# Small reciprocal-root chains on the Vector engine in other forms, and five instead of three output tiles multiplied in halves of the tokens at a change of stage

## The chip, the cores and the metric

The kernel runs on one core of a Trainium2 chip. The metric is the device time of one execution in microseconds (us). Five engines with a program each share the core's SBUF: TensorE (PE, with PEld for its weight loads), VectorE (DVE), ScalarE (ACT), GpSimd (POOL) and SyncE (SP, which issues transfers). PE writes its results to PSUM.

## The reference

512 tokens of width 1024 pass through two layers (mixer, then a feed-forward network) and a second block (attention, then a feed-forward network). All in fp32:

```python
def rms_norm(x, g):
    y = xf * lax.rsqrt(jnp.mean(xf * xf, axis=-1, keepdims=True) + EPS)
    return y * g
for l in range(2):
    h = rms_norm(x, g_pre_mix[l]) * (1 + sc_mix) + sh_mix
    x = x + gt_mix * rms_norm(mixer(h, ...), g_post_mix[l])
    h = rms_norm(x, g_pre_mlp[l]) * (1 + sc_mlp) + sh_mlp
    f = square(relu(h @ w_ff1[l])) @ w_ff2[l]          # 1024 -> 4096 -> 1024
    x = x + gt_mlp * rms_norm(f, g_post_mlp[l])
# second block
h = rmsnorm(x, attn_norm_w);  x = x + attention(h)
h2 = rmsnorm(x, mlp_norm_w);  x = x + square(relu(h2 @ w_up)) @ w_down
return rmsnorm(x, final_norm_w)
```

## The kernel before

**Products.** A product of fp32 matrices is made from three matmuls of rounded parts (`mm3`, L202 to L204): high by high, high weight by low activation, low weight by high activation. Weights come in chunks of 128x1024: a transfer into a raw buffer (`wr`, two of them), a rounded high part by ACT (L178), and the low part as the difference, by DVE in one piece or by POOL in four (L182). The pair goes to one of four `w` buffers. `W()` hands out the next chunk and prepares chunks up to four ahead; a fifth has to wait until the first of the four is used up.

**Change of stage.** A mixer or a feed-forward network ends in `tok_group`: four accumulators (tiles `p`), one for each group of 128 tokens, added to `E` by DVE as each gets its last product. Then `post_norm` takes the groups in pairs (or singly, where `pt=1`: the end of the first feed-forward network). For each pair: squares summed (ACT L580), multiplied by a gate row (POOL L582), a first chain of small DVE operations (`rsqrt`, all of it at L69 with tiles named `c`), the update `E += E*c` (DVE), squares again (ACT L593), a second chain, the scaling (ACT L460, DVE), 16 transposes on PE (L475) two blocks to a PSUM bank, eviction (DVE and ACT L485), and the split into high (ACT L214) and low parts (DVE) `hT`. The next stage multiplies weights by `hT`.

`rsqrt` is a bit-trick guess and two correction steps, in 128x`w` operations: `w` is 2 for a pair, 1 for a single group. A chain of `w=2` has 9 operations, one of `w=1` has 7.

**Halves.** At the head of a stage `feat` takes several output tiles of 128 columns at once:

```python
for _ in evacs: ws.append(self.W()...)
for i, _ in enumerate(evacs):
    bs.append(self.bank(tag="py" if halves and i >= 3 else tag))
for a, b in ([(0, 256), (256, 512)] if halves else [(0, 512)]):
    if a:
        self.work_off()                 # transposes of the second pair
    for w, p, ev in zip(ws, bs, evacs):
        for k in range(8):
            self.mm3(p[:, a:b], ...)    # 24 matmuls of 256 columns
```

so the first 256 tokens of all these tiles are multiplied before the second pair of groups is there. The number of tiles is `HALVES` in the three feed-forward networks (`self.feat([ev] * HALVES, halves)`) and in the second mixer; the first mixer and the second block begin otherwise. The remaining tiles are multiplied 512 tokens wide. A scheduler sorts the instructions of each engine from priorities and its own clock of the work issued, so that an edit also moves neighbours.

The five changes of stage are at 431 us (first mixer to first network), 807 (network to second mixer), 1197 (mixer to network), 1575 (network to second block) and 1977 (second block to last network).

Of the kernel before, what the change touches and what calls it, by code (L numbers as in the profile page):

```python
# [10 lines left out]
I32 = mybir.dt.int32  # L11
AFTER = mybir.DependencyInfo(mybir.DependencyClass.NoSync, mybir.DependencyReason.DATA)
AF = mybir.ActivationFunctionType
OP = mybir.AluOpType

T, D, DFF = 512, 1024, 4096
NL, NH, DH = 2, 4, 256
KC, KM = 31, 4
EPS = 1e-6
AHEAD = 4  # L20
HALVES = 3
MID = 3
PIECE = 256
CALM = True
# [22 lines left out]
RSQRT_C, RSQRT_GUESS = 1.5 ** 0.2, 0x5f05a21f  # L47
# [25 lines left out]
class Kern:  # L73
# [148 lines left out]
            nc.scalar.activation(hi, src, AF.Copy if isinstance(scale, float) else AF.Identity, scale=scale)  # L222
            self.V.scalar_tensor_tensor(lo, src, scale, f32(hi), op0=OP.mult, op1=OP.subtract)

    def rsqrt(self, src, w, mul, add, tag=None):

        V = self.V
        vh, z, q, y1, y = (self.c(w, tag) for _ in range(5))

        def half_square(z):  # L230
            a = self.c(w, tag)
            if w == 1:
                V.scalar_tensor_tensor(a, z, vh, z, op0=OP.mult, op1=OP.mult)
            else:
                V.tensor_tensor(a, z, z, op=OP.mult)
                V.tensor_tensor(a, a, vh, op=OP.mult)
            return a
        V.tensor_scalar(vh, src, 0.5 * mul, 0.5 * add, op0=OP.mult, op1=OP.add)
        V.tensor_scalar(z.bitcast(I32), vh.bitcast(I32), -0.5, RSQRT_GUESS, op0=OP.mult, op1=OP.add)
        h = half_square(z)  # L240
        V.scalar_tensor_tensor(q, h, -RSQRT_C ** 2 * 5 / 3, h, op0=OP.add, op1=OP.mult)
        V.scalar_tensor_tensor(y1, q, RSQRT_C ** 4 * 5 / 4, z, op0=OP.add, op1=OP.mult)
        a = half_square(y1)
        V.scalar_tensor_tensor(y, a, 1.5, y1, op0=OP.subtract, op1=OP.mult, reverse0=True)
        return y
# [199 lines left out]
        for ev, b in zip(evacs, bs):  # L445
            ev(b)

    def norm_T(self, ii, xs, ss, G, sh, to):

        V, w = self.V, len(xs)  # L450
        if ii == 0:
            self.new_hT()
        r = self.rsqrt(ss, w, 1.0 / D, EPS)
        for b in range(2):
            h = slice(512 * b, 512 * b + 512)
            for t in range(w):
                if (t if w > 1 else b):
                    V.tensor_scalar(to[t][:, h], xs[t][:, h], r[:, t:t + 1], None, op0=OP.mult)
                else:
                    self.nc.scalar.activation(to[t][:, h], xs[t][:, h], AF.Copy, scale=r[:, t:t + 1])  # L460
        self.xn += to
        if len(self.xn) == 2:
            i, x, self.xn = ii + w - 2, self.xn, []
            for q in range(4):
                self.pend.append((i, lambda q=q: self.norm_T2(i, q, x, G, sh)))
# [92 lines left out]
    def post_norm(self, l, which, nxt):  # L558

        nc, V = self.nc, self.V  # L560
        self.ada_wait(l, range(16 + 24 * which, 24 + 24 * which))
        row = self.gate_row(l, which)
        GS = nxt()
        self.n += 1
        dst = self.dram.tile([T, D], F32, name=f"xd{self.n}")
        src = self.xsrc
        self.xsrc = [dst[i * 128:(i + 1) * 128, :] for i in range(4)]
        xs, ss, w = [None] * 4, {}, 1 if self.tune["pt"] else 2

        def ready(i, nh):  # L570
            y, t = self.y[i], i % w
            self.calm = nh == 1 and CALM
            h = slice(nh * 512, (nh + 1) * 512)
            if nh == 0:
                xs[i] = self.tile("E", (128, D))
                nc.sync.dma_start(xs[i], src[i])
                if t == 0:
                    ss[i // w] = self.c(2 * w)
            with self.soon():
                nc.scalar.activation(self.tile("j", (128, 512), BF16), y[:, h], AF.Square,  # L580
                                     accum_out=ss[i // w][:, w * nh + t:w * nh + t + 1])
                nc.gpsimd.tensor_tensor(y[:, h], y[:, h], row[:, h], op=OP.mult)  # L582
            return (lambda: update(i - t)) if nh and t == w - 1 else None

        def update(i):
            with self.soon():
                s, s1, s2 = ss[i // w], self.c(w), self.c(w)
                V.tensor_tensor(s1, s[:, 0:w], s[:, w:2 * w], op=OP.add)
                r = self.rsqrt(s1, w, 1.0 / D, EPS)
                for t in range(w):  # L590
                    n, x = i + t, xs[i + t]
                    V.scalar_tensor_tensor(x, self.y[n], r[:, t:t + 1], x, op0=OP.mult, op1=OP.add)
                    nc.scalar.activation(self.y[n].bitcast(BF16)[:, 0:D], x, AF.Square, accum_out=s2[:, t:t + 1])  # L593
                    nc.sync.dma_start(self.xsrc[n], x)
                    self.dbg(f"x{l}{which}_{n}", x)
                self.norm_T(i, xs[i:i + w], s2, *GS, self.y[i:i + w])
        return ready


# [280 lines left out]
    def mixer(self, l, nxt, halves=True):  # L880
        nc, V = self.nc, self.V
        o, _ = COLS["w_conv_m"]
# [7 lines left out]
        def ev_xm(j):  # L890
            def ev(p):
                if j % 2 == 0:
                    xmt[j // 2], xct[j // 2] = (self.tile("E", (128, 2, T)) for _ in range(2))
                xm, xc = xmt[j // 2][:, j % 2], xct[j // 2][:, j % 2]
                nc.scalar.activation(xm, p, AF.Copy)
                y, th = p, self.t2()
                w = lambda d: self.cols[l][:, o + j * KM + KM - 1 - d:o + j * KM + KM - d]
                nc.scalar.activation(y, p, AF.Identity, scale=w(0), bias=self.col(l, "b_conv_m", j))
                for d in range(1, KM):
                    V.scalar_tensor_tensor(y[:, d:], xm[:, :T - d], w(d), y[:, d:], op0=OP.mult, op1=OP.add)  # L900
                nc.scalar.activation(th, y, AF.Tanh)
                V.scalar_tensor_tensor(xc, th, 1.0, y, op0=OP.add, op1=OP.mult)
            return ev
# [4 lines left out]
        def ev_gb(c):  # L908
            def ev(p):
                th = self.t2()  # L910
                nc.scalar.activation(th, p, AF.Tanh, scale=0.5)
                self.drain(lambda: c - self.taps_done < self.bufs["ga"])
                a = self.tile("ga", (128, T))
                V.scalar_tensor_tensor(a, th, 1.0, ga["a"], op0=OP.add, op1=OP.mult)
                inp[c] = a
            return ev
# [11 lines left out]
        glu = lambda c: self.feat([ev_ga]) or self.feat([ev_gb(c)])  # L928
        z = lambda j: self.feat([ev_z(j)])
        nh = HALVES  # L930
        gw = self.gate_weights(l)
        rest = lambda: [0 for _ in gw]
        if halves:
            next(gw), next(gw)
            self.feat([ev_xm(j) for j in range(nh)], halves, rest)
            glu(0)
        else:
            nh = 2
            self.start([ev_xm(0), ev_xm(1), ev_ga, ev_gb(0)])
            self.load_cols(1)  # L940
# [21 lines left out]
        hms, ss = [], {}  # L962
# [696 lines left out]
```

## Time and the profile before

| | |
|---|---|
| median of 3 runs | 2338.77 us (2337.93 to 2339.65) |
| profiled execution | 2338.5 us, of it the span 2336.8 us |
| PE busy | 2224.5 us, 95% of the span |
| DVE / ACT / POOL busy | 1484.2 / 972.6 / 709.3 us |
| granted TensorE clock, mean | 0.982 |

The profiled execution is a run of its own; its time is the span plus what lies before and after it. A row of a timeline gives start, duration, engine, line, operation, output and inputs with their shapes, and in brackets the idle time of the engine before it with what ended that. [...]

### The profile page before, as it was taken

To read this page: it belongs to the slowest core of one execution; us is meant where nothing else is said; L and a number is where in the kernel's file an instruction comes from. 1 tells how busy PE (TensorE), PEld (TensorE's weight loads), DVE (VectorE), ACT (ScalarE), POOL (GpSimd) and SP (SyncE) were. 2 spreads that over 40 slices of the span, in tenths; PEclk is the share of its full clock that TensorE was granted. 3 is DMA by queue.
4 is the path that set the end of the run, shared out by engine and by line. 5 is a ranking of instruction groups with operands and counts; after the bars stand their busy time and mean duration, and the time that the engine had idled before them with its cause. 6 is when DMAs were issued, how large, how long until landed. Compare 5 with 4: busy or idle time off the path is not lost.

```text
span 2336.8 us, 28930 instructions
## 1 busy us (share of the span) xinstructions
PE 2224.5 (95%) x10552; PEld 1811.9 (78%) x10552; DVE 1484.2 (64%) x2927; ACT 972.6 (42%) x1697; POOL 709.3 (30%) x934
## 2 busy tenths in 40 slices
PE   5998999799999999999989999998989999999998
PEld 3777887688888777788768888877878888888886
DVE  6698998645677669999663233346996435443434
ACT  3435554433232354555443323234447544332322
POOL 4645561425335254565341201212212330000000
PEclk9999999899999999999999999999999999999999
DMA  7524236336666433222333423323111234322232
GB/s 281 166 83 136 64 92 214 109 127 213 211 207 207 145 100 89 74 69 68 114 107 90 135 90 99 99 81 114 55 55 55 64 108 153 104 95 95 88 105 82
DMA packets 77758, 271.37 MB, mean 116 GB/s; under 512 B 9008, under 2 KB 9776, under 8 KB 77616
## 3 DMA queue, kind: packets, MB, share of 16 engines
q1 hardware_dynamic: 69840, 241.21, 32.1%
q0 software_dynamic: 7776, 28.32, 3.8%
q8 instruction: 83, 1.36, 0.2%
q14 instruction: 59, 0.48, 0.1%
HBM read 256.91 MB, written 12.58 MB: 115 GB/s over the span
## 4 chain that ended last, share of the span: by engine, by line
PE 75%; DVE 14%; ACT 4%; issue 2%; POOL 2%; DMA 1%; SPq 0%; ACTq 0%; DVEq 0%; POOLq 0%
PE p L202 23%; PE p L204 23%; PE p L203 23%; DVE p L839 3%; DVE c L69 3%; DVE E L69 1%; POOL w L182 1%; PE p L475 1%; DMA ad<-in_ada_dram 1%; DVE w L69 1%; DVE s L69 1%; ACT w L178 1%; PE p L621 1%; PE p L1211 1%; DVE hT L69 1%
## 5 line engine op out<-in xcount | busy, mean ns | idle before, releaser
L182 POOL TENSOR_TENSOR w<-wr,w 128x256 fp32r<-128x256 f32 x648 | 493.5, 794 | 722.1 <-ACT w L178 629.4
L178 ACT ACTIVATE w<-wr 128x1024 fp32r<-128x1024 f32 (+1 forms) x353 | 369.2, 1048 | 598.1 <-PE p L204 523.1
L202 PE MATMUL p<-hT,w 128*128 128x512 f32 (+1 forms) x1504 | 577.1, 385 | 15.4 <-ACT hT L214 7.3
L203 PE MATMUL p<-hT,w 128*128 128x512 f32 (+1 forms) x1504 | 573.0, 381 | 9.4 <-POOL hT L218 5.4
L204 PE MATMUL p<-hT,w 128*128 128x512 f32 (+1 forms) x1504 | 573.4, 382 | 1.5 <-POOL w L182 1.5
L202 PE MATMUL p<-w,s 128*128 128x512 f32 (+1 forms) x1152 | 450.8, 391 | 3.5 <-ACT s L214 3.5
L204 PE MATMUL p<-w,s 128*128 128x512 f32 (+1 forms) x1152 | 448.8, 390 | 0.6 <-DVE s L69 0.6
L203 PE MATMUL p<-w,s 128*128 128x512 f32 (+1 forms) x1152 | 448.5, 389 | 0.6 <-DVE w L69 0.6
L69 DVE TENSOR_TENSOR w<-wr,w 128x1024 fp32r<-128x1024 f32 (+1 forms) x187 | 233.0, 1247 | 290.9 <-ACT w L178 290.5
L202 PEld LDWEIGHTS p<-hT,w 128*128 128x128 f32 x1504 | 286.2, 191 | 74.7 <-ACT hT L214 9.6
L839 DVE SCALAR_TENSOR_TENSOR p<-ga,ad,p 128x495 f32<-128x495 f32 (+24 forms) x480 | 339.3, 728 | 6.6 <-ACT p L834 5.5
L203 PEld LDWEIGHTS p<-hT,w 128*128 128x128 f32 x1504 | 286.3, 190 | 67.3 <-POOL hT L218 6.5
L204 PEld LDWEIGHTS p<-hT,w 128*128 128x128 f32 x1504 | 286.1, 190 | 57.8 <-POOL w L182 3.8
L202 PEld LDWEIGHTS p<-w,s 128*128 128x128 f32 x1152 | 217.1, 188 | 52.1 <-ACT s L214 4.5
L204 PEld LDWEIGHTS p<-w,s 128*128 128x128 f32 x1152 | 217.0, 188 | 50.1 <-DVE s L69 1.5
L203 PEld LDWEIGHTS p<-w,s 128*128 128x128 f32 x1152 | 217.3, 189 | 49.3 <-DVE w L69 1.0
L69 DVE TENSOR_TENSOR E<-p,E 128x512 f32<-128x512 f32 (+4 forms) x152 | 94.8, 638 | 145.7 <-PE p L204 117.5
L69 DVE SCALAR_TENSOR_TENSOR t<-p,t 128x512 f32<-128x512 f32 x96 | 65.9, 687 | 127.8 <-ACT t L1033 127.8
L296 DVE SCALAR_TENSOR_TENSOR ad<-ad,ad 128x1024 f32<-128x1024 f32 x80 | 107.2, 1345 | 53.6 <-DMA ad<-in_ada_dram 53.6
L1033 ACT ACTIVATE t<-p 128x512 f32<-128x512 f32 x96 | 56.7, 590 | 163.7 <-PE p L204 163.7
L69 DVE TENSOR_TENSOR s<-t,s 128x512 fp32r<-128x512 f32 (+1 forms) x100 | 102.1, 1021 | 12.8 <-ACT s L1035 7.3
L582 POOL TENSOR_TENSOR E<-E,s 128x512 f32<-128x512 f32 x32 | 45.9, 1441 | 168.7 <-ACT j L580 168.7
(272 smaller groups left out, 2648.7 us busy)
## 6 DMA issues: line engine op xcount, KB each, us to landing
wr<-in_ff_dram SPq DMA_DIRECT2D x128, 512.0 KB, 3.8
wr<-in_win_dram SPq DMA_DIRECT2D x64, 512.0 KB, 3.8
ad<-in_ada_dram POOLq DMA_DIRECT2D x54, 512.0 KB, 4.8
wr<-in_wout_dram SPq DMA_DIRECT2D x40, 512.0 KB, 3.8
wr<-in_up_dram SPq DMA_DIRECT2D x32, 512.0 KB, 3.6
wr<-in_down_dram SPq DMA_DIRECT2D x32, 512.0 KB, 3.5
ad<-in_ada_dram SPq DMA_DIRECT2D x26, 512.0 KB, 4.6
xd<-E SPq DMA_DIRECT2D x20, 512.0 KB, 2.7
```

What stands on the lines that cost most here:

```text
L69: return f(out, *a, **kw)
L178: self.nc.scalar.activation(u[:, 0, :w], raw[:, :w], AF.Copy)
L182: self.nc.gpsimd.tensor_tensor(u[:, 1, o:e], raw[:, o:e], f32(u[:, 0, o:e]), op=OP.subtract)
L202: mm(out, lh, rh, start=first, stop=False)
L203: mm(out, lh, rl, start=False, stop=False)
L204: self.mm = mm(out, ll, rh, start=False, stop=last)
L296: return self.nc.vector.scalar_tensor_tensor(w, w, 1.0, self.cact, op0=OP.mult, op1=OP.mult, accum_out=m)
L475: nc.tensor.transpose(p[:, k, 128 * t:128 * t + 128], x[t][:, j * 128:(j + 1) * 128], self.ident)
L582: nc.gpsimd.tensor_tensor(y[:, h], y[:, h], row[:, h], op=OP.mult)
L621: nc.tensor.matmul(p[32 * h:32 * h + 32, (c // 2) * 256:(c // 2) * 256 + 256], wg[:, h, c, e, :], ws[3 * h + c][:, e, :], start=c != 1 and ...
L839: V.scalar_tensor_tensor(y[:, d:], a[:, :T - d], w[:, o - d:o - d + 1], y[:, d:], op0=OP.mult, op1=OP.add)
L1033: nc.scalar.activation(r, p, AF.Relu)
```

## The change

Three parts. `HALVES` goes from 3 to 5; the fourth and fifth tile get the two PSUM banks of tag `py`. In the second mixer the five are its three first tiles and the two that `glu(0)` made 512 wide after them. `rsqrt` gets a form for `w=1` in which every operation is a `tensor_scalar` with one tensor and per-partition scalars (7 operations as before), and a form for `w=2` in which three intermediate values lie in a PSUM bank (tag `pc`), so that each operation on two tensors has one of them in PSUM (10 operations for 9). `post_norm` uses the latter for both chains of its pairs; `add_norm` (second block to last network) doesn't pass `new` and keeps the old form.

```diff
-HALVES = 3
+HALVES = 5
-    def rsqrt(self, src, w, mul, add, tag=None):
+    def rsqrt(self, src, w, mul, add, tag=None, new=None):
+        if w == 1:
+            vh, z, h, q, y1, a, y = (self.c(w, tag) for _ in range(7))
+            ts = V.tensor_scalar
+            ts(vh, src, -0.5 * mul, -0.5 * add, op0=OP.mult, op1=OP.add)
+            ts(z.bitcast(I32), vh.bitcast(I32), -0.5, RSQRT_GUESS - 2 ** 30, op0=OP.mult, op1=OP.add)
+            ts(h, z, vh, z, op0=OP.mult, op1=OP.mult)
+            ts(q, h, RSQRT_C ** 2 * 5 / 3, h, op0=OP.add, op1=OP.mult)
+            ts(y1, q, RSQRT_C ** 4 * 5 / 4, z, op0=OP.add, op1=OP.mult)
+            ts(a, y1, vh, y1, op0=OP.mult, op1=OP.mult)
+            ts(y, a, 1.5, y1, op0=OP.add, op1=OP.mult)
+            return y
+        if new:
+            vh, a, h, q, b, c, y = (self.c(w, tag) for _ in range(7))
+            z, hp, y1 = (new() for _ in range(3))
+            tt, stt = V.tensor_tensor, V.scalar_tensor_tensor
+            V.tensor_scalar(vh, src, 0.5 * mul, 0.5 * add, op0=OP.mult, op1=OP.add)
+            V.tensor_scalar(z.bitcast(I32), vh.bitcast(I32), -0.5, RSQRT_GUESS, op0=OP.mult, op1=OP.add)
+            tt(a, vh, z, op=OP.mult)
+            tt(hp, a, z, op=OP.mult)
+            tt(h, a, z, op=OP.mult)
+            stt(q, hp, -RSQRT_C ** 2 * 5 / 3, h, op0=OP.add, op1=OP.mult)
+            stt(y1, q, RSQRT_C ** 4 * 5 / 4, z, op0=OP.add, op1=OP.mult)
+            tt(b, vh, y1, op=OP.mult)
+            tt(c, b, y1, op=OP.mult)
+            stt(y, c, 1.5, y1, op0=OP.subtract, op1=OP.mult, reverse0=True)
+            return y
...
+        scr = []
+        def new():
+            if not scr:
+                p = self.bank((128, 64, 8), "pc")
+                scr.extend(p[:, i, 0:w] for i in range(64))
+            return scr.pop()
...
-            self.feat([ev_xm(j) for j in range(nh)], halves, rest)
-            glu(0)
+            self.feat([ev_xm(j) for j in range(3)] + [ev_ga, ev_gb(0)], halves, rest)
+            nh = 3
```

How the instructions stand is read from the built programs. On PE, at the change from the first mixer to the first network: `p729` is the last accumulator of the mixer, `E579` to `E582` are the four groups of tokens, the tiles with `hT` are output tiles of the network (`w732`, `w734`, `w736` the first three, `w785` the fourth). Before:

```order
L204 MATMUL p729_3956<-w730_3957,s714_3897 128x512
L475 MATMUL p759_4135<-identr_82,E579_3181 128x128
...
L475 MATMUL p766_4175<-identr_82,E580_3182 128x128
L202 MATMUL p729_3956<-w730_3957,s715_3903 128x512
...
L204 MATMUL p792_4256<-hT749_4067,w736_3978 128x256
L475 MATMUL p793_4329<-identr_82,E581_3183 128x128
...
L475 MATMUL p799_4359<-identr_82,E582_3184 128x128
L202 MATMUL p790_4254<-hT749_4067,w732_3962 128x256
```

and now:

```order
L204 MATMUL p729_3956<-w730_3957,s714_3897 128x512
L202 MATMUL p729_3956<-w730_3957,s715_3903 128x512
...
L498 MATMUL p760_4138<-identr_82,E579_3181 128x128
...
L204 MATMUL p797_4277<-hT750_4069,w736_3978 128x256
L202 MATMUL p798_4278<-hT750_4069,w785_4235 128x256
...
L498 MATMUL p800_4400<-identr_82,E581_3183 128x128
...
L204 MATMUL p798_4278<-hT750_4069,w785_4235 128x256
...
L498 MATMUL p804_4420<-identr_82,E581_3183 128x128
...
L202 MATMUL p795_4275<-hT750_4069,w732_3962 128x256
```

The last three matmuls of `p729` stood behind the 16 transposes of the first pair and now stand ahead of them. Ahead of the second pair's first 8 transposes there are now 14 matmuls of the fourth tile, and 10 more between these and the other 8.

The fifth tile (`p799`, chunk `w787`) stands on PE at the same change only here, behind the second half of the first tile (`p795`) and ten matmuls of the second half of the second (`p796`):

```order
L204 MATMUL p795_4275<-hT750_4069,w732_3962 128x256
L203 MATMUL p796_4276<-hT751_4070,w734_3970 128x256
...
L203 MATMUL p796_4276<-hT751_4070,w734_3970 128x256
L202 MATMUL p799_4279<-hT750_4069,w787_4243 128x256
L203 MATMUL p799_4279<-hT751_4070,w787_4243 128x256
L204 MATMUL p796_4276<-hT750_4069,w734_3970 128x256
L204 MATMUL p799_4279<-hT750_4069,w787_4243 128x256
```

In the program before, no row of the fifth tile has 256 columns: there it is 512 wide and comes later. The change from the first network to the second mixer reads alike (the fourth tile's first half ahead of the gate weights' matmuls, the fifth behind the second half of the first tile), and so does the one from mixer to network at 1197 us; at the last change the 16 transposes keep their place and both new tiles come behind them.

On DVE, at the change from the second network to the second block, the second chain of the first pair before (`c2260`, `c2263`, `c2261` are its end, the tiles `w` are low parts of weights, `E1986` the scaling of the second group, `t` an eviction of transposes):

```order
L69 SCALAR_TENSOR_TENSOR c2260_13345<-c2259_13344,c2258_13343 128x2
L69 TENSOR_TENSOR c2263_13354<-c2260_13345 128x2
L69 TENSOR_TENSOR c2263_13354<-c2263_13354,c2257_13342 128x2
L69 SCALAR_TENSOR_TENSOR c2261_13346<-c2263_13354,c2260_13345 128x2
L69 TENSOR_SCALAR E1986_11402<-E2225_13193,c2261_13346 128x512
L69 TENSOR_TENSOR w2238_13244<-wr2221_13159,w2238_13244 128x1024
L69 TENSOR_TENSOR w2240_13249<-wr2237_13242,w2240_13249 128x1024
L69 TENSOR_SCALAR E1986_11402<-E2225_13193,c2261_13346 128x512
L69 TENSOR_TENSOR t2266_13413<-p2265_13408,ad1928_10980 128x512
```

and now (`p2257` is the PSUM bank of the chain, `c2266` its result, `E1990` the sum of the fourth group of tokens):

```order
L69 TENSOR_TENSOR c2262_13500<-c2261_13499,p2257_13479 128x2
L69 TENSOR_TENSOR w2240_13398<-wr2223_13313,w2240_13398 128x1024
L69 TENSOR_TENSOR w2242_13403<-wr2239_13396,w2242_13403 128x1024
L69 SCALAR_TENSOR_TENSOR c2263_13501<-p2257_13479,c2262_13500 128x2
L69 TENSOR_TENSOR E1990_11558<-p2237_13392,E1990_11558 128x512
L69 SCALAR_TENSOR_TENSOR p2257_13479<-c2263_13501,p2257_13479 128x2
L69 TENSOR_TENSOR c2264_13502<-c2260_13498,p2257_13479 128x2
L69 TENSOR_TENSOR c2265_13503<-c2264_13502,p2257_13479 128x2
L69 SCALAR_TENSOR_TENSOR c2266_13504<-c2265_13503,p2257_13479 128x2
L69 TENSOR_TENSOR c2277_13613<-c2230_13367 128x2
```

The low parts of two weight chunks stood behind the chain, between the two halves of a scaling; they now stand inside the chain, and so does the sum of the fourth group.

## Rows read from the trace of the kernel before

**Rows 1.** Timeline of PE at the change from first mixer to first network.

```profile
434.87 3.68 PE L475 MATMUL p<-identr,E 128*128 128x128 f32 x16 [3.38 <-ACT E L460]
...
440.24 0.69 PE L202 MATMUL p<-hT,w 128*128 128x256 f32 x2 [0.41 <-ACT hT L214]
...
451.19 0.28 PE L203 MATMUL p<-hT,w 128*128 128x256 f32 x1
451.31 0.28 PE L204 MATMUL p<-hT,w 128*128 128x256 f32 x1
...
456.00 1.97 PE L475 MATMUL p<-identr,E 128*128 128x128 f32 x8 [4.42 <-ACT E L460]
```

**Rows 2.** Timeline of DVE there: the second pair's first chain begins at 441.67.

```profile
429.31 0.38 DVE L69 TENSOR_SCALAR c<-c 128x2 f32<-128x2 f32 x2 [0.62 <-ACT E L593]
...
430.11 1.16 DVE L69 SCALAR_TENSOR_TENSOR c<-c 128x2 f32<-128x2 f32 x1
...
434.03 1.79 DVE L69 TENSOR_SCALAR E<-E,c 128x512 f32<-128x512 f32 x2
...
441.67 1.25 DVE L69 TENSOR_TENSOR c<-c 128x2 f32<-128x2 f32 x1
...
449.32 2.85 DVE L69 SCALAR_TENSOR_TENSOR E<-E,c,E 128x1024 f32<-128x1024 f32 x2
453.39 0.37 DVE L69 TENSOR_SCALAR c<-c 128x2 f32<-128x2 f32 x2 [1.22 <-ACT E L593]
...
455.16 0.88 DVE L69 TENSOR_SCALAR E<-E,c 128x512 f32<-128x512 f32 x2
```

**Rows 3.** Timeline of POOL there: low parts of weights, four pieces a chunk.

```profile
431.22 5.88 POOL L182 TENSOR_TENSOR w<-wr,w 128x256 fp32r<-128x256 f32 x8
...
443.44 6.46 POOL L182 TENSOR_TENSOR w<-wr,w 128x256 fp32r<-128x256 f32 x8 [0.53 <-ACT w L178]
```

**Rows 4.** Windows: stretch, its length, busy time of each engine, PEclk, DMA share, GB/s.

```profile
431.50:440.20 8.70, 4.96 (x19) 4.14 (x19) 6.51 (x11) 4.26 (x9) 5.59 (x8) 0.64 0.40 115
...
472.00:499.20 27.20, 27.20 (x121) 22.30 (x120) 11.39 (x14) 10.51 (x16) 8.78 (x11) 1.00 0.42 131
```

**Rows 5.** Groups of DVE by shape: count, busy us, mean ns of one.

```profile
L69 DVE TENSOR_TENSOR c<-c 128x4 f32<-128x4 f32 x20 | 3.1, 157 | 0.1
...
L69 DVE TENSOR_TENSOR d<-p,ga 128x16 f32<-128x16 f32 x2 | 0.3, 155 | 0.0
```

**Rows 6.** Timeline of PE at the change from mixer to network at 1197 us.

```profile
1200.83 2.75 PE L475 MATMUL p<-identr,E 128*128 128x128 f32 x16 [3.38 <-ACT E L460]
...
1221.01 1.97 PE L475 MATMUL p<-identr,E 128*128 128x128 f32 x8 [4.41 <-ACT E L460]
```

**Rows 7.** Timeline of PE at the change from network to second mixer.

```profile
812.15 1.03 PE L475 MATMUL p<-identr,E 128*128 128x128 f32 x6 [3.15 <-DVE c L69]
...
832.96 1.36 PE L475 MATMUL p<-identr,E 128*128 128x128 f32 x6 [2.22 <-ACT E L460]
```

**Rows 8.** Timeline of DVE there, two pieces of chains of single groups.

```profile
808.65 2.49 DVE L69 SCALAR_TENSOR_TENSOR c<-c,c 128x1 f32<-128x1 f32 x3
...
829.48 0.34 DVE L69 TENSOR_SCALAR c<-c 128x1 f32<-128x1 f32 x2 [1.22 <-ACT E L593]
```

**Rows 9.** Timeline of POOL there.

```profile
825.05 6.57 POOL L182 TENSOR_TENSOR w<-wr,w 128x256 fp32r<-128x256 f32 x8 [2.83 <-issue]
```

**Rows 10.** Timeline of PE at the changes at 1575 and 1977 us.

```profile
1576.07 0.88 PE L475 MATMUL p<-identr,E 128*128 128x128 f32 x6 [1.46 <-ACT E L460]
...
1977.64 1.09 PE L475 MATMUL p<-identr,ad 128*128 128x128 f32 x8 [2.18 <-ACT ad L460]
```

**Rows 11.** The page: costliest groups (busy us, mean ns, idle before) and DMA issues.

```profile
L178 ACT ACTIVATE w<-wr 128x1024 fp32r<-128x1024 f32 (+1 forms) x353 | 369.2, 1048 | 598.1 <-PE p L204 523.1
...
L69 DVE TENSOR_TENSOR w<-wr,w 128x1024 fp32r<-128x1024 f32 (+1 forms) x187 | 233.0, 1247 | 290.9 <-ACT w L178 290.5
...
wr<-in_ff_dram SPq DMA_DIRECT2D x128, 512.0 KB, 3.8
```

More of the change, by code (lines that the diff above doesn't have):

```diff
@@ L231, in half_square @@
             a = self.c(w, tag)
[L232 to L236, printed above, removed]
+            V.tensor_tensor(a, z, z, op=OP.mult)
+            V.tensor_tensor(a, a, vh, op=OP.mult)
             return a
@@ L446, in start, with norm_T @@
             ev(b)
-    def norm_T(self, ii, xs, ss, G, sh, to):
+    def norm_T(self, ii, xs, ss, G, sh, to, new=None):
         V, w = self.V, len(xs)
@@ L452, in norm_T @@
             self.new_hT()
-        r = self.rsqrt(ss, w, 1.0 / D, EPS)
+        r = self.rsqrt(ss, w, 1.0 / D, EPS, new=new)
         for b in range(2):
@@ L587, in update @@
                 s, s1, s2 = ss[i // w], self.c(w), self.c(w)
-                V.tensor_tensor(s1, s[:, 0:w], s[:, w:2 * w], op=OP.add)
-                r = self.rsqrt(s1, w, 1.0 / D, EPS)
+                if w == 1:
+                    V.tensor_scalar(s1, s[:, 0:1], s[:, 1:2], None, op0=OP.add)
+                else:
+                    V.tensor_tensor(s1, s[:, 0:w], s[:, w:2 * w], op=OP.add)
+                r = self.rsqrt(s1, w, 1.0 / D, EPS, new=new)
                 for t in range(w):
@@ L595, in update @@
                     self.dbg(f"x{l}{which}_{n}", x)
-                self.norm_T(i, xs[i:i + w], s2, *GS, self.y[i:i + w])
+                self.norm_T(i, xs[i:i + w], s2, *GS, self.y[i:i + w], new)
         return ready
```

## The prediction

> **What bounds the kernel now.** I read the engines' busy time first: PE is busy for 2224.5 of 2336.8 us, so PE's program is the bound, and what an edit can win is PE time lost at some place: idle, or run at the lower clock. The timeline of PE with its idle times shows that the longest losses lie at the changes of stage. At the first (431 us) [rows 1] PE waits 3.38 us for the scaling of the first pair, then, after the first 256 tokens of three tiles, 4.42 us for that of the second pair. The change at 1197 us repeats it almost to the digit [rows 6]. From network to second mixer it is 3.15 and 2.22 us [rows 7], at the last two changes 1.46 and 2.18 [rows 10]. Around such a wait the clock is low too: 0.64 over 431.5 to 440.2, where PE was busy for 4.96 of 8.70 us [rows 4].
>
> What the waits hang on is seen in DVE's timeline beside POOL's. The first pair's second chain begins at 429.31 and ends at 434.03 [rows 2]: 4.7 us for nine operations. The same chain for the second pair, with POOL silent, runs from 453.39 to 455.16: 1.77 us, 0.197 an operation. In the first case a single 128x2 operation takes 1.16, and POOL is making low parts of weights from 431.22 to 437.1, 0.74 a piece [rows 3]: the chain goes on at POOL's pace. The first chain of the second pair lies under the next eight pieces (443.44 to 449.9) and needs 441.67 to 449.32.
>
> **First change of stage, chains.** Do operations with one operand in PSUM escape POOL, and what do they cost? The trace of before has no such 128x2 chain. The nearest rows: an add of PSUM and SBUF with 16 elements takes 155 ns, one of two SBUF tensors with 4 elements, mostly away from POOL, 157 [rows 5]. So I take the uncontended 0.197 an operation, 10 operations, 1.97 us; the other bound is the old 4.7. Operations with a scalar and one SBUF tensor (the first of the chain) stay as they are.
>
> [...]
>
> With 0.197 the second chain ends at 431.3 rather than 434.0. PE by then has its last three matmuls of the mixer ahead of the transposes (0.7 us; they stood behind them), ends at 432.2 and finds the scaling done: the transposes start at 432.2, not 434.87, without a wait. From the start of the transposes to the first product of the network it is 5.37 us before [rows 1], part of it at clock 0.64 and part the three matmuls; so that product comes at 437.6 if nothing else gets better, at 436.3 if the 16 transposes run in some 2 us at the full clock. That is 2.6 to 3.9 us earlier than 440.24. Low parts of `hT` still come late as before.
>
> **First change, second pair.** The sum of the last accumulator now stands ahead of the evictions, and the first chain of the second pair no longer goes at POOL's pace; it ends near 440.3 (scaling until 431.3 + 1.8, the sum 0.7 behind it, a square, then evictions and splits between the operations) rather than 449.32. The two updates `E += E*c` keep two operands in SBUF. They took 2.85 [rows 2], and POOL's next eight pieces, now some 3 us earlier (440 to 446.5), will lie on them. Done at 443.2 if POOL doesn't touch them, at 444.7 if each waits for a piece, at 447.8 if they have to wait for the end of POOL. From there to the transposes it was 3.9 us (squares, the uncontended chain, scaling: 452.1 to 456.0): 447.1, 448.6 or 451.7.
>
> PE meanwhile has 72 matmuls as before (440.24 to 451.4: 11.2 us), and now 14 of the fourth tile at 0.12 us [rows 1], 1.7: busy until 449.2 to 450.5. The second transposes therefore come between 449.2 and 451.7, 4.3 to 6.8 us earlier than 456.0. Besides, 24 matmuls of the fourth tile (2.8 us) are by then behind PE or fill the gap between the two groups of transposes; before they came later, at their full price. If PE stays busy its clock doesn't fall, and the transposes (8 in 1.97 at 456.00, 8 in 1.09 at 1977 [rows 1, 10]) are up to 1.7 us shorter.
>
> **The fifth tile.** Its weights need the buffer that the first tile frees, so it stands behind the first tile's second half: it covers nothing, effectively four tiles are ahead. It costs a wait: the high part takes ACT 1.05 [rows 11], ten matmuls (1.2) lie ahead; then POOL gives a piece each 0.74 for six matmuls of 0.12. Bounds 0.3 and 1.5; I take 0.8.
>
> Sum for this change: 4.3 to 6.8, plus 2.8, plus 0 to 1.7, less 0.3 to 1.5: 5.6 to 11.0. I take **8**, below the middle, since new small waits (after the first transposes for the first `hT`) will hold the clock down a little. That the gain isn't given back: the stage behind has PE busy for 27.20 of 27.20 us at clock 1.00 [rows 4].
>
> **Mixer to network at 1197 us:** same code, same waits [rows 6]: **8**.
>
> **Network to second mixer.** The chains are 128x1. Three operations on two tensors take 2.49 us at 808.65, beside POOL; two operations with scalars alone take 0.34 at 829.48, in the middle of POOL's pieces (825.05 to 831.6) [rows 8, 9]: that form isn't held up. Seven of them are 1.2 us, and the chain at 808 ends 2.0 us earlier. PE has ten matmuls (1.2 us) more ahead of the second group's transposes; 2.0 + 1.2 covers the 3.15. The second wait, 2.22, is covered by 11 more matmuls of the third tile and 24 of the fourth (4.1 us). 5.37 in all, up to 1 of clock, less 0.8 for the fifth tile. If only the chains count it is 3. I take **5**.
>
> [...]
>
> **Network to second block (1575 us).** No halves here. The low parts of two weight chunks (1.25 each [rows 11]) and a sum (0.7) stand inside the first pair's second chain now: its end, and so the transposes, up to 3.2 us later. Given back: one operation that POOL held up (1 us), and an earlier sum for the second pair. Bounds −4 and +1; I take **−1.5**.
>
> **Second block to last network (1977 us).** The chain is the old one and its 2.18 us wait [rows 10] stays, since both new tiles come behind the transposes. Only the fifth tile's wait is added, 0 to 1.5: **−0.5**.
>
> **Rest.** 192 more matmuls, because 8 tiles are now multiplied in halves, at next to the same columns: 0.3. The four chains of the final norm, of which one ends the program: seven operations of 0.17 against the like before, ±0.2. Together **−0.5**.
>
> 8 + 8 + 5 − 1.5 − 0.5 − 0.5 = 18.5 us. The profiled execution took 2338.5, 0.3 below the median of the runs: **2320.0**.
>
> **The rivals.**
> *Only the chains gain.* The fourth tile's weights come too late to fill anything (its low part comes from the last four of POOL's eight pieces, 446.5), or the second pair is ready before PE has done its 72: then of 8 there remain 5 to 5.5 at both changes, 3 at the second mixer: 13.5 − 2.5 = 11, **2327.5**. For it: the order shows 24 matmuls only between two kinds of transposes. Against: 446.5 is ahead of 447.5, the earliest end of the third tile.
> *The block moves to the updates.* They wait for POOL's end in both changes, as computed (451.7): 6 rather than 8 each, 4 of the 5, less 2.5: 13.5, **2325**. This is the upper end of my forecast.
> *The new operations are dearer.* If one with a PSUM operand takes a third more than 0.197, a chain is 0.65 us longer; two at each pair's way to the transposes, at three changes, of which the cover hides none: some six chains count, 4 us, **2324**. [...]
> *The scalar form is held up by POOL after all,* in the middle of its seven operations: the 2.0 us at the second mixer stay lost, **2322**. [...]
> *The fifth tile stops PE: slower.* If its raw weights weren't in SBUF when the buffer comes free, PE would wait for transfer, high part and pieces, 3.8 + 1.05 + 3.0 [rows 11], less 1.2: 6.6 us at four places, 26.5 against the 21.7 that the sum has without that wait: **2343**. It decides from 5.4 us a place on. Against it: the raw buffer of that chunk comes free when POOL ends its eight pieces (449.9 before, earlier now), and 3.8 us later is still ahead of the first tile's second half.
> *Given back.* A later stage runs into something else (DVE's convolution in the second mixer, weights), so that PE idles there: **2334** or more. The window at 472 to 499 speaks against it for the networks; for the second mixer I have no such row.
>
> **Chances and range.** The forecast, 2314 to 2325 with the block at the updates: 0.50. Dearer operations 0.05, the scalar form held up 0.03, both inside that stretch. Chains only, 2325 to 2331: 0.23. Given back, 2331 to 2338: 0.09. Fifth tile stops PE: 0.05. Better than 2314: 0.05. A measurement here tells 0.2%, 4.7 us, from no change, so faster (below 2334): 0.50 + 0.05 + 0.03 + 0.23 + 0.05 + a third of 0.09 = 0.89; same 0.07; slower 0.04. Range 2312 to 2331.
>
> **What would show it.** In the trace after: chains of ten 128x2 operations in about 2 us with POOL busy; no wait of 3.38 ahead of the first transposes, and the second pair's transposes 17 to 19.5 us behind the mixer's last matmul, not 24.5; an idle time under 1.5 us at the fifth tile's first matmul; transposes at 1576 some 2 us later, counted from the end of the network's products. The forecast is wrong if operations with PSUM still take 0.65 beside POOL, if the updates of `E` stretch until POOL is done, or if PE stands still at the fifth tile by more than 5 us.

## The result, and the profile after

The changed kernel takes 2314.48 us (median of 4 runs, 2312.6 to 2317.1) against 2338.35 (4 runs): a ratio of 0.9899, 95% interval 0.9887 to 0.9911. The profiled execution took 2312.6, its span is 2310.9 us: 25.9 less than before. A second set of runs gave 2315.63 and a ratio of 0.991 (0.9896 to 0.9924).

PE at the first change of stage, in the timeline that answers to [rows 1]:

```profile
432.05 1.97 PE L498 MATMUL p<-identr,E 128*128 128x128 f32 x16 [0.43 <-ACT E L483]
...
435.55 0.50 PE L202 MATMUL p<-hT,w 128*128 128x256 f32 x2 [1.53 <-ACT hT L214]
436.65 0.39 PE L203 MATMUL p<-hT,w 128*128 128x256 f32 x1 [0.61 <-DVE hT L69]
...
448.64 1.09 PE L498 MATMUL p<-identr,E 128*128 128x128 f32 x8
...
450.85 1.09 PE L498 MATMUL p<-identr,E 128*128 128x128 f32 x8
...
453.74 0.39 PE L203 MATMUL p<-hT,w 128*128 128x256 f32 x1 [0.98 <-DVE hT L69]
...
457.92 0.39 PE L202 MATMUL p<-hT,w 128*128 128x256 f32 x1
...
458.73 0.38 PE L204 MATMUL p<-hT,w 128*128 128x256 f32 x1 [0.19 <-POOL w L182]
...
460.57 0.38 PE L204 MATMUL p<-hT,w 128*128 128x256 f32 x1 [0.17 <-POOL w L182]
```

The waits of 3.38 and 4.42 us are 0.43 and none. A new one of 1.53 stands ahead of the first product of the network, as PE is now done with the transposes before `hT` is there. The last three rows are the fifth tile's. The idle times given for them add up to 0.36 us. Counted from start to start they cost more: matmuls of this width start 0.12 us apart elsewhere, and these three start 0.30, 0.46 and 0.45 after the one before, together 0.85 us late.

DVE there, as in [rows 2]:

```profile
428.91 0.17 DVE L69 TENSOR_SCALAR c<-c 128x2 f32<-128x2 f32 x1 [0.62 <-ACT E L626]
429.11 0.16 DVE L69 TENSOR_SCALAR p<-c 128x2 int32<-128x2 int32 x1
...
429.70 0.16 DVE L69 TENSOR_TENSOR c<-c,p 128x2 f32<-128x2 f32 x1
...
430.67 0.16 DVE L69 SCALAR_TENSOR_TENSOR c<-c,p 128x2 f32<-128x2 f32 x1
430.86 1.85 DVE L69 TENSOR_SCALAR E<-E,c 128x512 f32<-128x512 f32 x2
...
435.76 1.98 DVE L69 TENSOR_TENSOR hT<-t,hT 128x512 fp32r<-128x512 f32 x2
...
441.06 0.16 DVE L69 SCALAR_TENSOR_TENSOR c<-c,p 128x2 f32<-128x2 f32 x1
441.32 3.31 DVE L69 SCALAR_TENSOR_TENSOR E<-E,c,E 128x1024 f32<-128x1024 f32 x2
445.85 0.17 DVE L69 TENSOR_SCALAR c<-c 128x2 f32<-128x2 f32 x1 [1.22 <-ACT E L626]
...
447.61 0.16 DVE L69 SCALAR_TENSOR_TENSOR c<-c,p 128x2 f32<-128x2 f32 x1
```

and POOL, as in [rows 3]:

```profile
429.57 1.29 POOL L612 TENSOR_TENSOR E<-E,s 128x512 f32<-128x512 f32 x1 [6.22 <-ACT j L610]
430.82 6.37 POOL L182 TENSOR_TENSOR w<-wr,w 128x256 fp32r<-128x256 f32 x8
...
439.04 8.28 POOL L182 TENSOR_TENSOR w<-wr,w 128x256 fp32r<-128x256 f32 x8 [0.16 <-ACT w L178]
```

The second chain of the first pair runs from 428.91 to 430.83, 1.92 us instead of 4.72, while POOL multiplies the gate row from 429.57 on: no operation waits. The second pair's second chain takes the same 1.92 us (445.85 to 447.77), and it lies under POOL's pieces of low parts until 447.32. What still has two operands in SBUF still meets POOL, and more than before: two low parts of `hT` take 1.98 rather than 1.28 (at 440.47 before), the updates of `E` 3.31 rather than 2.85, and POOL's eight pieces 8.28 instead of 6.46.

The windows (stretch, its length, busy time of PE, PEld, DVE, ACT, POOL, then PEclk, DMA share, GB/s) show the clock, to be held against [rows 4]:

```profile
431.50:440.00 8.50, 5.93 (x35) 5.14 (x35) 8.40 (x18) 6.68 (x13) 8.34 (x11) 0.84 0.39 120
440.00:449.00 9.00, 8.87 (x73) 8.67 (x72) 6.92 (x19) 4.51 (x7) 7.32 (x8) 0.96 0.47 159
449.00:460.00 11.00, 9.72 (x75) 8.74 (x74) 5.92 (x10) 6.72 (x12) 2.06 (x3) 1.00 0.18 65
```

It is 0.84 in the first stretch, where it was 0.64. The second pair's transposes ran at 456.00 before, in a stretch at 0.61:

```profile
452.00:463.00 11.00, 5.42 (x22) 4.65 (x23) 6.00 (x19) 6.70 (x14) 0.00 (x0) 0.61 0.39 136
```

Now they lie in the stretches at 0.96 and 1.00.

### The profile page after: what moved, and what is told of

Its sections match the earlier page's. It is cut to its first block, busy times and chain, and to the rows that moved or that the text cites. A ratio compares the mean times of both kernels' runs of the same rounds, so it can differ in the third digit from the quotient of the medians.

```text
span 2310.9 us, 29330 instructions
## 1 busy us (share of the span) xinstructions
PE 2217.4 (96%) x10744; PEld 1813.1 (78%) x10744; DVE 1470.7 (64%) x2939; ACT 972.4 (42%) x1697; POOL 718.9 (31%) x934
## 4 chain that ended last, share of the span: by engine, by line
PE 77%; DVE 10%; ACT 4%; POOL 3%; issue 3%; DMA 2%; SPq 0%; ACTq 0%; POOLq 0%; DVEq 0%
PE p L202 24%; PE p L204 24%; PE p L203 24%; DVE p L872 2%; POOL w L182 2%; DVE c L69 1%; ACT w L178 1%; DVE E L69 1%; DVE w L69 1%; DMA ad<-in_ada_dram 1%; PE p L1244 1%; DVE cc L69 1%; DMA wr<-in_win_dram 1%; DVE s L69 1%; DVE e L1276 1%
## 5 line engine op out<-in xcount | busy, mean ns | idle before, releaser
L182 POOL TENSOR_TENSOR w<-wr,w 128x256 fp32r<-128x256 f32 x648 | 502.6, 808 | 699.2 <-ACT w L178 619.1
L202 PE MATMUL p<-hT,w 128*128 128x512 f32 (+1 forms) x1568 | 586.6, 376 | 16.2 <-ACT hT L214 9.8
L203 PE MATMUL p<-hT,w 128*128 128x512 f32 (+1 forms) x1568 | 584.6, 373 | 9.2 <-POOL hT L218 5.4
L204 PE MATMUL p<-hT,w 128*128 128x512 f32 (+1 forms) x1568 | 585.0, 374 | 0.8 <-POOL w L182 0.7
L202 PE MATMUL p<-w,s 128*128 128x512 f32 (+1 forms) x1152 | 449.2, 390 | 3.5 <-ACT s L214 3.5
L202 PEld LDWEIGHTS p<-hT,w 128*128 128x128 f32 x1568 | 297.2, 190 | 72.5 <-ACT hT L214 11.6
L203 PEld LDWEIGHTS p<-hT,w 128*128 128x128 f32 x1568 | 298.3, 190 | 64.4 <-POOL hT L218 6.5
L204 PEld LDWEIGHTS p<-hT,w 128*128 128x128 f32 x1568 | 298.5, 190 | 56.0 <-POOL w L182 3.7
L69 DVE TENSOR_TENSOR s<-t,s 128x512 fp32r<-128x512 f32 (+1 forms) x100 | 99.2, 992 | 11.1 <-ACT s L1068 5.7
```

The source lines that it names most:

```text
L69: return f(out, *a, **kw)
L182: self.nc.gpsimd.tensor_tensor(u[:, 1, o:e], raw[:, o:e], f32(u[:, 0, o:e]), op=OP.subtract)
L202: mm(out, lh, rh, start=first, stop=False)
L203: mm(out, lh, rl, start=False, stop=False)
L204: self.mm = mm(out, ll, rh, start=False, stop=last)
```

## Where the time came from

To see the gain by stage I put numbered instructions of both traces beside each other (the n-th rounding of a weight chunk by ACT, the n-th eviction 512 wide from PSUM to a tile `t` by ACT, called tile n here, those of the mixers included) and took start after minus start before; the change of this offset over a stage is what the stage gained. For the changed kernel the offset is −0.20 at weight 49 (366 us before), −11.34 at tile 25 (494), the same at tile 49 (760), −15.61 at weight 169 (1137), −25.40 at tile 77 (1315), −25.78 at tile 97 (1514), −27.39 at weight 277 (1866), −25.93 at the end. So in us, all kernels against the one profile of before:

```
                        366-494  760-1137  1137-1315  1514-1866  1866-end
                        mixer->  network-> mixer->    network->  last
                        network  mixer 2   network    block 2    network
changed kernel           -11.1     -4.3      -9.8       -1.6       +1.5
changed kernel, again    -10.2     -5.1      -9.2       -2.0       +2.2
chains alone              -7.6     -8.0      -6.0       -2.5       +0.5
five halves alone         -3.5     +4.3      -4.2       -0.2       +0.7
three values in SBUF      -1.7     -4.6      -3.5       -1.5       +0.9
old single chain         -10.4     +4.3      -9.8       -1.3       +2.9
mixer's head as before    -9.9     -7.3     -10.1       -0.3       +1.4
four halves              -12.0     -8.5     -10.5       -2.4       +1.6
four halves, again       -11.9     -6.0     -10.3       -2.7       +2.8
four, last network three -12.0     -7.2     -10.3       -0.5       +2.2
four, old chain 1575     -12.0     -7.3      -9.8       -3.0       +2.6
four, priority 1575      -11.4     -7.1     -10.5       -1.7       +1.5
```

Each row is one execution. The two rows of one kernel differ by up to 2.5 us in a stage, so a smaller difference counts only where several rows repeat it.

## The experiments

**Chains alone, halves alone, the chain in SBUF, four halves.** Four kernels, timed beside each other. In the first, `HALVES = 3` and the second mixer's head as before the change; in the second, the chains of before:

```diff
-HALVES = 5
+HALVES = 3
-            self.feat([ev_xm(j) for j in range(3)] + [ev_ga, ev_gb(0)], halves, rest)
+            self.feat([ev_xm(j) for j in range(3)], halves, rest)
+            glu(0)
```

> The new chain forms alone: three tiles in halves, and the second mixer as before the change. Theory: the chains free the path and the fourth tile's halves only fill what is left, some 3 us at each of the two changes from mixer to network and 1 to 2 at the second mixer: 2319 to 2323 us, with PE waiting 2 to 3 us ahead of the second pair's transposes at the first change of stage. Rival (cover first: what counts is the work on PE ahead of the transposes, not the chains): 2329 or more, with waits near those of before.

Measured: 2317.87 us (5 runs), ratio 0.9911 (0.9898 to 0.9925). The chains alone give nearly all, and the time lies under the expected 2319 to 2323: their part of the gain had been put too low. In its PE timeline the second pair's transposes wait 1.95 us:

```profile
431.52 1.96 PE L498 MATMUL p<-identr,E 128*128 128x128 f32 x16 [0.44 <-ACT E L483]
...
448.10 1.09 PE L498 MATMUL p<-identr,E 128*128 128x128 f32 x8 [1.95 <-ACT E L483]
```

> Five tiles in halves alone, all chains in the old forms. The transposes of the first pair again stand ahead of the last three matmuls of the mixer, and only ten matmuls of the fourth tile come between the second pair's transposes. Theory (chains first): the waits of 3.4 and most of 4.4 us stay, 2331 to 2336 us. Rival (cover first): 2320 to 2326, with the wait ahead of the second pair's transposes below 2 us.

Measured: 2334.76 us (12 runs), ratio 0.9985 (0.9973 to 0.9997). Halves without the chains are worth next to nothing in sum. The waits are where they were; the two changes from mixer to network still gain 3.5 and 4.2 us in the table, and at the second mixer the kernel loses 4.3.

```profile
433.82 3.44 PE L475 MATMUL p<-identr,E 128*128 128x128 f32 x16 [3.38 <-ACT E L460]
...
454.24 1.97 PE L475 MATMUL p<-identr,E 128*128 128x128 f32 x8 [4.16 <-ACT E L460]
```

The third puts the pair's three values back into SBUF, with the ten operations kept:

```diff
-            z, hp, y1 = (new() for _ in range(3))
+            z, hp, y1 = (self.c(w, tag) for _ in range(3))
```

> The change as it is, but the three values that the pair's chain keeps in PSUM lie in SBUF: ten operations, the same in all else. Theory (PSUM is what frees the chain from GpSimd): the chain ahead of the first transposes again takes over 4 us, single operations over 0.6 us beside GpSimd's pieces, 2328 to 2336 us. Rival (the other grouping of the operations or the order that comes with it does it): the chain takes about 2 us, 2313 to 2318.

Measured: 2330.75 us (6 runs), ratio 0.9963 (0.995 to 0.9977). DVE's chain ahead of the first transposes takes 428.49 to 433.87, 5.4 us, with POOL beside it (the gate row from 429.15, its pieces from 430.40). PE waits 4.13 and 4.37 us ahead of the two pairs' transposes.

```profile
428.49 0.37 DVE L69 TENSOR_SCALAR c<-c 128x2 f32<-128x2 f32 x2 [0.61 <-ACT E L626]
428.90 1.56 DVE L69 TENSOR_TENSOR c<-c,c 128x2 f32<-128x2 f32 x3
430.49 1.33 DVE L69 SCALAR_TENSOR_TENSOR c<-c,c 128x2 f32<-128x2 f32 x2
431.86 1.33 DVE L69 TENSOR_TENSOR c<-c,c 128x2 f32<-128x2 f32 x2
433.22 0.65 DVE L69 SCALAR_TENSOR_TENSOR c<-c,c 128x2 f32<-128x2 f32 x1
```

Same operations, same count: the place of one operand decides. With it the order went back as well (the mixer's last three matmuls behind the transposes, one matmul of the fourth tile ahead of the second pair's transposes), since the scheduler's own reckoning also follows the form. So the 9.4 us between 1.7 and 11.1 at the first change are chain and order together; the chain's own part is the 3.5 us between 5.4 and 1.9.

The fourth takes four tiles; in the second mixer `ev_gb(0)` is multiplied 512 wide after them:

```diff
-HALVES = 5
+HALVES = 4
-            self.feat([ev_xm(j) for j in range(3)] + [ev_ga, ev_gb(0)], halves, rest)
+            self.feat([ev_xm(j) for j in range(3)] + [ev_ga], halves, rest)
+            self.feat([ev_gb(0)])
```

> The change with four tiles in halves instead of five (in the second mixer the first half of the gate pair's second tile goes, too). Theory (the fifth tile stands behind the first tile's second half and covers nothing): within 2 us of the changed kernel, 2312 to 2317 us. Rival (the fifth tile still fills waits in the second halves): 2319 or more.

Measured: 2310.32 us (4 runs), ratio 0.9877 (0.9862 to 0.9892); once more 2312.73 and 0.9886 (0.9871 to 0.9901). The expected 2312 to 2317 was missed on the fast side the first time. The fifth tile covers nothing, and the kernel is faster without it: its eight runs took 2307.66 to 2313.7, mean 2311.2, the eight of the changed kernel 2312.6 to 2318.05, mean 2315.2. The two were not timed beside each other, and single intervals overlap, so 4 us is rough. In the table the networks' changes differ by about 1 us, within what one kernel's rows differ; the second mixer differs by 1 to 4.

**The single chains; the second mixer; the last network.** Again timed beside each other, with the changed kernel.

> The changed kernel once more, beside the three that follow: 2313 to 2317 us if the time of record is right.

Measured: 2315.63 us (4 runs), ratio 0.991.

The next has only the `w=1` chains in their old form, with the sum of a group's two squares ahead of them:

```diff
-        if w == 1:
+        if w == 0:
...
-        if new:
+        if new and w == 2:
...
+            if w == 1:
+                V.scalar_tensor_tensor(a, z, vh, z, op0=OP.mult, op1=OP.mult)
+            else:
...
-                if w == 1:
+                if w == 0:
                     V.tensor_scalar(s1, s[:, 0:1], s[:, 1:2], None, op0=OP.add)
```

> The change with the chains of single groups in their old form (change from the first network to the second mixer, and the final norm). Theory (the scalar form escapes GpSimd, and the second mixer starts the earlier for it): slower than the changed kernel by 5 to 9 us, 2320 to 2324 us, the loss all between 780 and 1150 us. Rival (five tiles in halves cover this change by themselves): within 2 us of the changed kernel.

Measured: 2324.15 us (5 runs), ratio 0.9943 (0.9931 to 0.9955). 8.5 us more than the changed kernel beside it. In the profiles it loses 8.6 and 9.4 of that between 760 and 1137 us (+4.3 for −4.3 and −5.1), and some 1 us in the last stage. The PE timeline has the waits of [rows 7] again:

```profile
802.25 0.87 PE L501 MATMUL p<-identr,E 128*128 128x128 f32 x6 [3.15 <-DVE c L69]
822.87 0.88 PE L501 MATMUL p<-identr,E 128*128 128x128 f32 x6 [2.07 <-ACT E L486]
```

In the changed kernel they are 0.21 and 0.41, and DVE's chain there, beside POOL from 796.37 on, isn't held up:

```profile
795.71 0.34 DVE L69 TENSOR_SCALAR c<-c 128x1 f32<-128x1 f32 x2 [0.62 <-ACT E L626]
796.09 0.27 DVE L69 TENSOR_SCALAR c<-c,c 128x1 f32<-128x1 f32 x1
796.39 0.21 DVE L69 TENSOR_SCALAR c<-c 128x1 f32<-128x1 f32 x1
796.64 0.78 DVE L69 TENSOR_SCALAR c<-c,c 128x1 f32<-128x1 f32 x3
```

```profile
796.37 1.30 POOL L612 TENSOR_TENSOR E<-E,s 128x512 f32<-128x512 f32 x1 [5.17 <-ACT j L610]
797.62 7.63 POOL L182 TENSOR_TENSOR w<-wr,w 128x256 fp32r<-128x256 f32 x8
```

The mixer's head as before the change, with five halves in the networks:

```diff
-            self.feat([ev_xm(j) for j in range(3)] + [ev_ga, ev_gb(0)], halves, rest)
+            self.feat([ev_xm(j) for j in range(3)], halves, rest)
+            glu(0)
             nh = 3
```

> The change with the second mixer's head as before it (three tiles in halves, the gate pair 512 wide), five in the networks. Theory (the mixer is held by VectorE from its first tap to its last, and the five tiles let that begin a microsecond later): 2 to 4 us faster than the changed kernel, 2310 to 2313 us. Rival (the four or five tiles in the mixer are a gain like in the networks): 2316 or more.

Measured: 2312.67 us (5 runs), ratio 0.9901 (0.9887 to 0.9915); 3 us under the changed kernel beside it, with intervals that overlap. What holds the second mixer was looked for in a window from the first to the last tap of its convolution. Before:

```profile
866.30:1137.00 270.70, 266.47 (x1333) 215.85 (x1333) 257.97 (x585) 136.84 (x263) 146.43 (x222) 1.00 0.26 78
```

After:

```profile
850.60:1121.40 270.80, 264.60 (x1321) 214.81 (x1320) 258.15 (x585) 136.66 (x263) 147.01 (x223) 0.99 0.24 77
```

Both are 271 us long. PE counts as busy for 98% of them and DVE for 95%, so by these rows either could hold the mixer. What speaks for DVE: after, 12 matmuls fewer lie in the stretch (they stand ahead of it), and it is no shorter; PE idles in it for 6.2 us instead of 4.2. That DVE holds the mixer is argued, not shown: no run changes DVE's work there. If it does, a gain ahead of this mixer counts as far as the first tap comes earlier. That tap stands, in the DVE timelines of the changed kernel and of this experiment, at

```profile
850.58 3.12 DVE L872 SCALAR_TENSOR_TENSOR p<-ga,ad,p 128x511 f32<-128x511 f32 x4 [2.31 <-ACT p L867]
```

```profile
849.04 2.33 DVE L872 SCALAR_TENSOR_TENSOR p<-ga,ad,p 128x511 f32<-128x511 f32 x3 [1.28 <-ACT p L867]
```

With the offsets at 760 us taken off (−11.34 and −9.51), the first tap is 4.4 us earlier than before (866.27) with five tiles and 7.7 with the old head: the gate pair's tiles, of which the taps live, come 3.3 us later when they are drawn into the halves. The stage's gains, 4.3 and 7.3, follow that. The kernels with four tiles don't: their first tap is 4.1 to 5.5 us earlier than before, and they gain 6.0 to 8.5, because from first to last tap they take 268.4 to 269.7 us and all the others 270.7 to 272.0. So the table shows that the fifth tile costs some 3 us at the second mixer; why it does is not settled.

Three tiles in halves in the last network, four elsewhere:

```diff
-                self.feat([ev] * HALVES, halves)
+                m = 3 if onto_x else HALVES
+                self.feat([ev] * m, halves)
...
```

> Four tiles in halves, but three in the last network, where the transposes of the second pair stand ahead of the added tiles. Theory (there the added halves cover nothing and cost about 1 us, as the offsets of the four-tile kernel against the kernel before show): 1 us faster than four everywhere, 2308 to 2311 us. Rival: the same as or slower than four everywhere, 2311 or more.

Measured: 2310.72 us (4 runs), ratio 0.9889 (0.9876 to 0.9902): no gain over four everywhere, and the last stage loses 2.2 us in its profile as others do. The time lies in the range of the theory, but the stage doesn't bear it out: nothing here ties the loss to the added halves.

**The change of stage at 1575 us.** Four halves as the base, beside it the same with `post_norm`'s old chain at this one change, and with a priority of 200 for the post-norm there.

> Four tiles in halves once more, as the base of the two that follow: 2308 to 2313 us if its first time holds.

Measured: 2312.73 us (4 runs).

```diff
-        def new():
+        def fresh():
             if not scr:
...
             return scr.pop()
+        new = None if l == 1 and which == 1 else fresh
```

> Four tiles in halves, and at the change from the second network to the second block the pair's chains in their old form, so that the low parts of two weight chunks stand behind the chain again. The prediction's term (the new order loses 1.5 us there): 1 to 2 us faster than four tiles alone, the wait ahead of the first transposes back from 2.8 to 1.5 us. Rival (what the second pair gains outweighs it, as in the offsets of the changed kernel): 1 to 3 us slower, with a wait of 2.4 us ahead of the second pair's transposes again.

Measured: 2310.51 us (4 runs), ratio 0.9885 (0.9869 to 0.9902). No difference outside the intervals. The waits are those of before, 1.47 ahead of the first transposes and 2.40 ahead of the second:

```profile
1546.39 0.87 PE L498 MATMUL p<-identr,E 128*128 128x128 f32 x6 [1.47 <-ACT E L483]
...
1564.09 1.53 PE L498 MATMUL p<-identr,E 128*128 128x128 f32 x12 [2.40 <-ACT E L483]
```

while the changed kernel has 2.83 at the first and none at the second:

```profile
1552.30 0.44 PE L498 MATMUL p<-identr,E 128*128 128x128 f32 x2 [2.83 <-ACT E L483]
...
1568.46 1.47 PE L498 MATMUL p<-identr,E 128*128 128x128 f32 x12
```

```diff
-        dict(slack=10.0, tap=1500, prep=-30, fetch=0, ada=0, aq=0, ak=1, af=1, bp=0, pt=0, adma=100, gap=3.0, pool=('01', '1'), mv=(), early=0, pin=0, go=0, ho=1),
+        dict(slack=10.0, tap=1500, prep=-30, fetch=0, ada=0, aq=0, ak=1, af=1, bp=200, pt=0, adma=100, gap=3.0, pool=('01', '1'), mv=(), early=0, pin=0, go=0, ho=1),
```

> Four tiles in halves, new chains everywhere, and at the end of the second network a priority of 200 instead of 0 for the post-norm's instructions: the sum of the fourth group now stands behind the chain, and the two low parts of weights one operation apart near its end. Theory (what delays the first transposes are the 2.5 us of low parts inside the chain): they are still inside it, the wait stays 2 to 3 us, within 2 us of four tiles alone. Rival (the sum and the place of the later low parts count): 2 us or more faster.

Measured: 2309.76 us (4 runs), ratio 0.9883 (0.9863 to 0.9904). The wait is 2.50. The median is 3 us under the base's, as the rival had it, but the intervals overlap and the table shows no more gain in that stage (−1.7 beside −2.4 and −2.7): undecided.

## Why the prediction was right, and where its terms were off

**The mechanism** is as forecast. The small chains went at POOL's pace (4.72 us for a pair's nine operations at the first change); with an operand in PSUM ten take 1.92 beside POOL, at 128x1 three operations with only scalars beside one tensor 0.78 where three on two tensors took 2.49, and the three-values-in-SBUF kernel (5.4 us for the ten) shows that nothing else in the pair's new form does it. The measured gain, 23.9 us of the median, lies above the 18.5 of the sum; 2314.48 is within the range, near its lower end. By the table the sum was 2 to 3 us short at the first change, 1 to 2 at 1197 and 3 at 1575, and too high by 1 to 2 in the last stage. It also divided the gain wrongly: the rival *only the chains gain* put the chains alone at 11 us, and they give 20.6.

**First change and the one at 1197 us: 8 each forecast, 10.2 to 11.1 and 9.2 to 9.8 measured.** The order of steps held: chain of ten in 1.92 (1.97 forecast), transposes at 432.05 (432.2), first product at 435.55 (436.3 to 437.6), second transposes at 448.64 (449.2 to 451.7). The term that was too small is the clock: I put it at 0 to 1.7 us and took less, since new small waits would "hold the clock down a little". From 366 to 494 the same columns kept PE busy for 112.0 us before and 108.5 after, at a mean granted clock of 0.93 and 0.99; its idle time fell from 16.0 to 8.4. At 1197 us (1137 to 1315) it is 164.9 and 162.0 busy, 13.1 and 6.2 idle. So 3.5 and 2.9 us of the two gains are busy time. The updates of `E` did meet POOL, as the rival had it, but that cost them 0.5 us more than before, and they didn't wait until POOL was done. Chains alone are 7.6 and 6.0 of it, the fourth tile's halves 2.6 to 3.8 (2.8 forecast).

**Second mixer: 5 forecast, 4.3 and 5.1 measured; the number came out by luck.** The waits that I counted went as forecast (3.15 and 2.22 to 0.21 and 0.41), and yet two terms were wrong. The chains alone win 8.0 here, where the rival "if only the chains count" had 3. The change ends a third wait of 1.00 us too (0.23 now), which I hadn't counted; PE's busy time at the same columns falls by 1.0 us in the changed kernel (365.6 to 364.6), where I gave the clock up to 1. The five tiles, which I counted as a gain, take some 3 us of it back. The scalar form is worth about the same with either head: 8.0 us with three tiles (chains alone), 8.6 and 9.4 with five (+4.3 against −4.3 and −5.1); five tiles cost 4.3 with the old form and 3 to 4 with the new.

**Network to second block: −1.5 forecast, no loss measured.** The first transposes are later, as the order said (2.83 for 1.46), but the second pair's wait is gone, and old and new chain give the same time. The table has gains of 1.6 and 2.0, above my upper bound of 1, and one of 3.0 with the old chain, so they aren't the new chain's; the profiles don't settle the size. The sign I took from the first pair alone.

**Fifth tile: 0.8 forecast at each change; at the first 0.36 us idle, 0.85 by the starts.** So the price was right there. It buys nothing: four tiles beat five.

**Last stage: −0.5 forecast, 1.5 to 2.2 lost in the profiles of the changed kernel.** Kernels with three halves there lose 0.5 to 2.2 too, so the cause stays open; single profiles of one kernel (four, four again) differ by 1.2 in it.

**PSUM as an operand** costs nothing here. The groups of DVE by shape, after:

```profile
L69 DVE TENSOR_SCALAR c<-c,c 128x1 f32<-128x1 f32 x48 | 11.7, 243 | 1.6
L69 DVE TENSOR_TENSOR c<-c,p 128x2 f32<-128x2 f32 x48 | 7.5, 157 | 1.6
...
L69 DVE TENSOR_TENSOR p<-c,p 128x2 f32<-128x2 f32 x12 | 2.0, 166 | 0.4
```

157 and 166 ns stand beside 157 for two SBUF operands away from POOL [rows 5]. The rival *the new operations are dearer* put a third on 0.197 an operation; no run shows that third, and the chain of ten took 1.92 us where 1.97 was forecast. The scalar form was priced at 0.17 an operation; with scalars that are read per partition it is 0.24, and the chain 1.7 us, not 1.2. Where nothing contends it is even dearer than the old form: the last chain of the program takes 1.74 us from its first operation to the scaling behind it, and took 1.47; from the end of PE's last matmul to the end of the span it is 8.51 us, and was 8.24. A hold-up of the scalar form by POOL, the other rival, doesn't show at 128x1: three such operations took 0.78 at 796.64 with POOL at work, and 0.77 in the program's last chain. At 128x2 an operation with one SBUF tensor and scalars was held up (1.17 us, last section).

## What to carry to other kernels

Where a chain of tiny VectorE operations stands on the way to the next matmul while GpSimd works on large tiles, look at the duration of one: if it is near that of the GpSimd operation beside it (here 1.16 us beside a gate row of 1.29, 0.65 beside pieces of 0.74, and 0.16 with GpSimd silent), put one of its two operands into PSUM (0.16 to 0.17 beside GpSimd here), or use a form with one tensor and scalars (0.17 to 0.28 at 128x1; at 128x2 one took 1.17). Filling a wait with work taken from behind it paid here only as far as that work's operands could be ready (four buffers, so four tiles: 2311.2 us in the mean of eight runs, 2315.2 with the fifth), and it pays only if the stage behind doesn't lose by it, as the second mixer lost some 3 us with the fifth tile. The saving is to be read stage by stage: here a single number hid a gain of 8 and the loss of 3 of it at the same place.

## What the runs showed that I had not expected

An operation of 128x2 that uses SBUF alone was still held up, small as it is. The first operation of a pair's chain (128x2, SBUF to SBUF) takes 1.17 us at 422.20 in the changed kernel's DVE timeline, while POOL works from 422.05 on; the next, which writes to PSUM when POOL is done, 0.16. The 128x1 operations above, beside a gate row from 796.37 to 797.67, took 0.20 to 0.26 each.

```profile
422.20 1.17 DVE L69 TENSOR_SCALAR c<-c 128x2 f32<-128x2 f32 x1
423.40 0.16 DVE L69 TENSOR_SCALAR p<-c 128x2 int32<-128x2 int32 x1
```

```profile
422.05 1.29 POOL L612 TENSOR_TENSOR E<-E,s 128x512 f32<-128x512 f32 x1 [1.22 <-ACT j L610]
```

The hold-up is mutual: with the chains out of its way, DVE's large operations on two SBUF tensors come to lie on POOL's pieces; two low parts of `hT` take 1.98 us, 1.28 before, and eight pieces 8.28, 6.46 before. And two executions of one program differ stage by stage: the four-halves kernel gained 8.5 and 6.0 us at the second mixer in two profiles, and its eight transposes at the last change took 1.09 us in one and 1.97 in the other, after waits of 1.35 and 2.05:

```profile
1946.58 1.09 PE L498 MATMUL p<-identr,ad 128*128 128x128 f32 x8 [1.35 <-ACT ad L483]
```

```profile
1950.82 1.97 PE L498 MATMUL p<-identr,ad 128*128 128x128 f32 x8 [2.05 <-ACT ad L483]
```

The wait before them doesn't decide it: after one of 2.03 us they took 1.09 with the chains alone, and after one of 2.18 the same 1.09 before the change [rows 10]. A difference of a microsecond or two in one stage needs more than one profile.
